# Two-layer hybrid transformer on one core: where modulation is made, and how the last feed-forward chunk fetches and stores its residual

## The chip, the core and the metric

The kernel runs on one NeuronCore of one Trainium2 chip. The metric is the device time of one execution in microseconds (us); the kernel before has a median of 1690.97 us over three runs (1690.32 to 1692.22).

## The reference

Two consecutive layers act on 512 latent tokens and 256 context tokens of width 1024. Every layer does, for both streams,

```python
h = rms_norm(x) * (1 + scale1) + shift1
x = x + gate1 * (attention(h) @ w_out)
h = rms_norm(x) * (1 + scale2) + shift2
x = x + gate2 * (silu(h @ w_gate) * (h @ w_up)) @ w_down
...
out = rms_norm(x_latent) * final_norm
```

The six vectors shift, scale and gate of each layer (called components 0 to 5: shift1, scale1, gate1, shift2, scale2, gate2) are products of a conditioning vector, passed through SiLU, with a 1024 x 6144 matrix. The latent tokens use the vector c (v = 0 in the kernel), the context tokens c_ctx (v = 1). Layer 0 has multi-head latent attention and 2-D neighbourhood attention side by side; layer 1 has sliding-window attention. Only the latent tokens leave layer 1, so in layer 1 the context tokens give keys and values and no more.

## The kernel before

**Layout.** Activations lie transposed: feature on the partitions, token on the free axis. The residual is eight tiles (m = 0 to 7) of 128 features by 768 tokens, of which `LATS` is the first 512 columns and `CTXS` the last 256. The matmuls reach fp32 accuracy by splitting each operand into a rounded part and a remainder: `load_w` (L300) loads weights into a "wr" buffer by SP's queue, ScalarE casts them to "wh" (L305), VectorE or, where the planner's table says so, GpSimd subtracts to get "wl" (L306), and `mm3` (L309) does three matmuls for each pair of tiles (L315 to L317). There are three buffers each of wr, wh and wl, 24 of "b" (768 columns wide), eight of "p", and four each of "ph" and "pl".

**Order.** A scheduler that simulates a time line orders the instructions of each engine; each engine then executes its own list in order. Where no engine is given, `dma` issues on SP's queue, and SP waits in order for whatever a transfer needs, with all later transfers behind it. L133 is the line of that helper, so all such issues have it.

**Modulation.** `mod_tile` (L204) makes one of the eight 128-feature parts of a component. In its late form it loads a 512 KB tile into the only buffer "rope0" and takes one pass of VectorE for each conditioning vector (L214, a multiply with a running sum, and a short read of the sum). `mods_pe` (L178) makes a whole component with TensorE: for each of four steps eight matmuls of 128x256 with a 32-column stationary operand (L190), a copy by ScalarE (L192), two matmuls that pick the two vectors (L194) and two small additions on VectorE (L198). Its weights come in 256 KB loads. `PE_MODS` lists the components that take this way. All other parts are in one queue: of layer 0 the components 2, 4, 3 and 5, then of layer 1 the components 1, 0 and 2, 4, 3, 5. `bg(n)` (L289) makes the next n units of that queue where the program has it; `mod(...)` (L294) makes units until the wanted one is there. `BG` says how many units are made after each tile: `BG[1]` in layer 0's feed-forward (3 for the first four pairs, then 2), `BG[2]` in layer 0's output projection (1 for each latent tile), `BG[3]` in the last feed-forward projections. `DBG` is the pace of such units during layer 0's projections.

**Norm and output projection.** `output` (L1079) loops over two token ranges (latents, then context) and over the eight tiles: load weights, multiply, add to the residual (`add_residual`, L1058), square on ScalarE (L347) and add the squares on VectorE or GpSimd (L350). `rstd` (L353) then sums over the partitions with TensorE (L360), takes the root (L361) and reciprocal (L362), spreads it over a diagonal (L363), broadcasts it with TensorE (L368) and copies it (L369); after that each tile is scaled and shifted (L382 on VectorE, L383 on ScalarE, L384 on VectorE) for the projections that follow. While the second range runs, the first range's norm is taken in steps.

**Layer 0's feed-forward.** `ffn0` (L1255) goes in chunks over pairs j of the hidden dimension. `first_pair` (L1239) does j = 0 in plain form; from j = 1 `Pair` (L1183) uses a scheme with fewer products, with sums of weights made on VectorE (L1199 to L1207, casts L1179, remainders L1180, products and corrections L1217 to L1236). `head`, `body` and `tail` of successive pairs overlap. After each chunk the down projection adds into the residual, which between chunks lies in DRAM as `home[m]`: fetched whole (384 KB), added to, and stored whole.

**The last chunk** calls `output` and writes eight new "b" tiles: since `dst` is given, the latent columns are re-ordered while they are added, by eight small instructions per tile (L1071); the context columns take one (L1066). The old residual is fetched by `fetched` (L1074) at each use: for each tile the latent columns first (256 KB), later the context columns (128 KB), into a "p" buffer. After `ffn0`, the latent columns of each new tile are stored to DRAM (`parked`, L1324 to L1329, 256 KB each); they are read back (L1400 to L1404) for layer 1's output projection. Layer 1's K and V projections come right behind the last chunk (again L315 to L317), and the scheduler interleaves them with it. Since the fetches, the stores and the weights all go by SP's queue, their order there is the scheduler's.

Of the kernel before, what the change touches and what calls it, by code (L numbers as in the profile page):

```python
# [16 lines left out]
KT = D // P  # L17
NL = 512
NX = 256
NT = NL + NX  # L20
# [9 lines left out]
LATS = slice(0, NL)  # L30
CTXS = slice(NL, NT)
HT = NT // 2
TOK1, TOK2 = slice(0, HT), slice(HT, NT)
# [13 lines left out]
QF = 0  # L47
LQ, EACH = 50, 0
NR = "nb"
PE_MODS = ((0, 1), (0, 4))  # L50
SCALES = (2, 0, 1, 0, 1, 0, 0, 0)
KEEP = 1
OUTQ = 1
E0, E1, EF = 1, 1, 1
ORDER = ("2", "n3", "m", "")
AFTER = "012k5678"
DBG = 0.35
KC = (0, 1, 0)
C1 = 0
VP = 0  # L60
# [7 lines left out]
LOWER = 150  # L68
LOE = {(0, 2, 0): None, (0, 2, 1): None, (0, 5, 0): None, (0, 5, 1): 1, (1, 2, 0): None, (1, 2, 1): None, (1, 5, 0): None, (1, 5, 1): None}
PATTERN = ("fbsfbsfbbsfs",) * 3  # L70
BG = ((0, 0, 0, 0, 0), (3, 2), (1, 0), (0, 0))
FIRST = 2000
STEPS = ((2, 3, 4, 4), 5, 3)
HALVES = (slice(0, 256), slice(256, 512))
# [25 lines left out]
def hybrid_kernel(ctx: ExitStack, tc, I, out):  # L100
# [17 lines left out]
    def B(dt=F32, tag="b"):  # L118
        return T(tag, [P, NT], dt)
# [12 lines left out]
    def dma(o, i):  # L132
        return nc.sync.dma_start(f(o), f(i))  # L133

    V, S, G, PE = nc.vector, nc.scalar, nc.gpsimd, nc.tensor
# [153 lines left out]
    def bg(n=1):  # L289

        for _ in range(n):
            next(mods, None)
# [758 lines left out]
    H = []  # L1051
    for k in range(KT):
        t = B()
# [17 lines left out]
            V.scalar_tensor_tensor(d[:, n], o[:, b].rearrange("p (r c) -> p r c", r=8), g,  # L1071
                                   base[:, b].rearrange("p (r c) -> p r c", r=8), op0=ALU.mult, op1=ALU.add)

    def fetched(m, c):  # L1074
        t = B(tag="p")
        dma(t[:, c], home[m][:, c])
        return t

    def output(src, mov, l, comp, streams, norm, units, dst=None, keep=False, base=None):  # L1079

        rest, kept = iter(()), []
        for i, (c, v) in enumerate(streams):
            for m in range(KT):
                w = kept[m] if keep and i else load_w(src(m), len(mov), P, LOE[l, comp, i], "b" if keep else None)
                if keep and i == 0:
                    kept.append(w)
                o = banks([c], PG)
                mm3(o, w, mov)
                add_residual(m, o[0][0], l, comp, v, c, dst and dst[m], base and base(m, c))
                if c is TOK1:  # L1090
                    dma(home[m], H[m])
                norm.add(m, c)
                next(rest, None)
                bg(units[i])
            for _ in rest:
                pass
            rest = norm.rest(norm.acc, c, v)
        for _ in rest:
            pass

    STREAMS0 = ((LATS, 0), (CTXS, 1))
# [63 lines left out]
    norm, ops, sums = combined(H, 0, 3)  # L1165
# [12 lines left out]
    def parts(t, h, lo):  # L1178
        S.copy(h, t)  # L1179
        V.tensor_tensor(lo, t, f(h), op=ALU.subtract)  # L1180
        return h, lo
# [57 lines left out]
    def first_pair(tag):  # L1239

        dst, s = [B(F32R, tag) for _ in range(2)], B(tag="p")
        ws = [load_w(I["w_gu"][0, 0, i], KT, P) for i in range(2)]
        for c, a in ((TOK2, ("12", "22")), (TOK1, ("11", "21"))):
            for i, (h, lo) in enumerate(ws):
                o = PG()[:, :HT]
                for n, k in enumerate((0, 4, 1, 5, 2, 6, 3, 7)):
                    three(o, (h[:, k], lo[:, k]), ops[a[k // 4]][k % 4], n == 0, n == 7)
                if i == 0:
                    S.activation(s[:, c], o, AF.Silu)
                else:  # L1250
                    V.tensor_tensor(s[:, c], s[:, c], o, op=ALU.mult)
                    parts(s[:, c], *(x[:, c] for x in dst))
        return dst

    def ffn0(new, norm):  # L1255
        tags = ("st", "st", "b", "b")
        for ci, (k0, kc) in enumerate(CHUNKS0):
            hs, last = [], None
            for j in range(k0, k0 + kc):
                if j == 0:  # L1260
                    hs.append(first_pair(tags[0]))
                    for _ in sums():
                        pass
                else:
                    p = Pair(j, tags[j - k0])
                    p.head()
                    if last:
                        last.tail()
                    p.body()
                    hs.append(p.dst)  # L1270
                    last = p
                bg(BG[1][j >= 4])
            last.tail()
            src = lambda m: I["w_dn"][0, m, :, k0 * P : (k0 + kc) * P]
            if ci < len(CHUNKS0) - 1:
                for m in range(KT):
                    t = fetched(m, slice(0, NT))
                    o = banks((LATS, CTXS), PG)
                    mm3(o, load_w(src(m), kc, P), hs)
                    for i, (x, c) in enumerate(o):  # L1280
                        add_residual(m, x, 0, 5, i, c, None, t)
                    dma(home[m], t)
            else:
                new.extend(B() for _ in range(KT))
                output(src, hs, 0, 5, STREAMS0, norm, BG[3], new, False, fetched)

    def ffn(l, a, streams, new, norm):
        wide = [c for c, _ in streams] if l == 0 else [LATS]
# [30 lines left out]
    new = []  # L1319
    norm, A = modulated(new, 1, 0, G if E0 else None)  # L1320
    ffn0(new, norm)
    H = new


    parked = []
    for k in range(KT):
        t = dr.tile([P, NL], F32, name=f"parked{k}")
        dma(t, H[k][:, LATS])
        parked.append(t)  # L1329
    rope1 = T("rope0", [P, 2, NL])  # L1330
    dma(rope1, I["rope1"])
# [68 lines left out]
    H = []  # L1400
    for k in range(KT):
        t = B()
# [3 lines left out]
    norm, a = modulated(H, 1, 3, G if E1 else None)  # L1406
# [113 lines left out]
```

## Time and profile before

| what | value |
|---|---|
| median of the runs | 1690.97 us |
| profiled execution | 1692.46 us |
| its span in the profile | 1690.7 us |
| mean granted TensorE clock | 0.969 |

The profile has one execution on one core. PE is TensorE's matmuls, PEld its weight loads, DVE is VectorE, ACT ScalarE, POOL GpSimd, SP the engine that issues most transfers; PEq, SPq and the like are what an engine's sequencer does. A line of a time line has the start in us, the duration in us, the engine, the line of the kernel, the operation, output and inputs with the names of their buffers, the shape, the number of instructions taken together (x), and in brackets how long the engine stood idle before it and who ended that. A line of waits gives the waiting engine and line, the releaser, the sum in us, the number of waits and the longest. PEclk is the clock that was granted to TensorE, 1.00 being full speed.

### The profile page before, as it was taken

Reading aid. Unit: us, or ns where it says so; the run is one execution under the profiler, and the core shown is the slowest. Engines: PE = TensorE matmul, PEld = TensorE weight load, DVE = VectorE, ACT = ScalarE, POOL = GpSimd, SP = SyncE. Lnnn points to the kernel's source line nnn. Section 1 sums busy time; section 2 is a strip of 40 time slices with the busy share of each in tenths; the row PEclk is TensorE's granted clock in tenths of the full one; section 3 lists DMA queues with packets and bytes.
Section 4 is the critical chain, followed back from the end, with each engine's and each line's share of the span. In section 5 each row is a group of like instructions: output and inputs, shape, how many; then the busy total and the mean of one; then the engine's idle time right before and its main releaser. Section 6 shows DMA issues by size and latency. Waiting matters only on the chain. (4 is left out here: it accounts for less than half of the span.)

```text
span 1690.7 us, 24474 instructions
## 1 busy us (share of the span) xinstructions
PE 1565.4 (93%) x9110; PEld 1351.1 (80%) x9110; DVE 1116.0 (66%) x2241; ACT 751.2 (44%) x1466; POOL 257.7 (15%) x192
## 2 busy tenths in 40 slices
PE   4899989999887899999999994799999999999997
PEld 3587767777787789999999994587879888888887
DVE  5994878576889778675858673658887533343435
ACT  5453576675354324242424332447865422222223
POOL 1552722320000000000000003275003000000002
PEclk8899999999998999999999997799999999999999
DMA  9444232004641374646464634332005223232322
GB/s 326 159 152 157 77 109 71 22 6 150 203 171 56 124 280 161 214 142 224 150 215 144 246 122 143 101 100 88 2 2 172 90 83 117 83 104 82 110 70 90
DMA packets 82896, 216.36 MB, mean 128 GB/s; under 512 B 10069, under 2 KB 17753, under 8 KB 82777
## 3 DMA queue, kind: packets, MB, share of 16 engines
q1 hardware_dynamic: 81624, 213.75, 38.4%
q8 instruction: 71, 1.16, 0.3%
q10 hardware_dynamic: 1152, 1.05, 0.2%
q14 instruction: 49, 0.39, 0.1%
HBM read 188.55 MB, written 23.07 MB: 125 GB/s over the span
## 5 line engine op out<-in xcount | busy, mean ns | idle before, releaser
L305 ACT CAST wh<-wr 128x1024 fp32r<-128x1024 f32 (+4 forms) x183 | 156.8, 865 | 393.8 <-PE pss L316 100.7
L306 DVE TENSOR_TENSOR wl<-wr,wh 128x1024 fp32r<-128x1024 f32 (+4 forms) x172 | 182.2, 1065 | 134.5 <-ACT wh L305 131.7
L350 POOL TENSOR_TENSOR p<-p,p 128x256 f32<-128x256 f32 (+1 forms) x42 | 44.9, 1068 | 1131.0 <-DVE wl L306 649.8
L316 PE MATMUL psd<-b,wh 128*128 128x512 f32 (+3 forms) x388 | 139.4, 360 | 3.3 <-DVE b L1180 2.0
L315 PE MATMUL psd<-b,wh 128*128 128x512 f32 (+3 forms) x356 | 131.1, 369 | 7.7 <-DVE b L1066 5.3
L316 PE MATMUL pss<-b,wh 128*128 128x512 f32 (+3 forms) x394 | 136.0, 346 | 1.8 <-DVE b L384 1.8
L317 PE MATMUL psd<-b,wl 128*128 128x512 f32 (+3 forms) x356 | 129.0, 362 | 0.0
L518 ACT ACTIVATE p<-p,sm 128x512 f32<-128x512 f32 (+3 forms) x144 | 105.1, 730 | 35.6 <-DVE sm L522 33.3
L317 PE MATMUL pss<-b,wl 128*128 128x512 f32 (+3 forms) x338 | 119.8, 355 | 0.0
L315 PE MATMUL pss<-b,wh 128*128 128x512 f32 (+3 forms) x338 | 119.6, 357 | 0.0
L214 DVE CUSTOM_DVE_ANT_0 p<-rope,cond 128x1024 bf16<-128x1024 f32 x80 | 96.0, 1221 | 27.6 <-DMA rope<-in_mod_w_dram 27.3
L316 PE MATMUL pst<-b,wh 128*128 128x512 f32 (+2 forms) x274 | 94.5, 345 | 0.2 <-DVE b L1180 0.2
L316 PEld LDWEIGHTS psd<-b,wh 128*128 128x128 f32 (+1 forms) x388 | 73.1, 189 | 15.3 <-DVE b L384 3.3
L315 PE MATMUL pst<-b,wh 128*128 128x512 f32 (+2 forms) x234 | 84.1, 360 | 0.7 <-ACT b L1179 0.7
L317 PE MATMUL pst<-b,wl 128*128 128x512 f32 (+2 forms) x234 | 83.4, 357 | 1.1 <-DVE wl L306 1.1
L315 PEld LDWEIGHTS psd<-b,wh 128*128 128x128 f32 (+1 forms) x356 | 67.2, 189 | 20.7 <-ACT b L383 8.2
L316 PEld LDWEIGHTS pss<-b,wh 128*128 128x128 f32 (+1 forms) x394 | 74.3, 189 | 11.1 <-DVE b L384 2.0
L512 PE MATMUL pso<-ph,b 128*64 128x256 f32 (+1 forms) x384 | 77.9, 361 | 3.5 <-DVE ph L450 3.5
L512 PE MATMUL pso<-pl,b 128*64 128x256 f32 (+1 forms) x384 | 77.3, 360 | 0.2 <-DVE pl L450 0.2
L315 PE MATMUL pst<-st,wh 128*128 128x256 f32 (+2 forms) x161 | 55.2, 343 | 22.4 <-DVE b L1071 21.9
L315 PE MATMUL pss<-st,wh 128*128 128x512 f32 (+2 forms) x217 | 74.3, 342 | 1.4 <-ACT st L339 1.4
L317 PEld LDWEIGHTS psd<-b,wl 128*128 128x128 f32 (+1 forms) x356 | 67.3, 189 | 9.6
(462 smaller groups left out, 4561.8 us busy)
## 6 DMA issues: line engine op xcount, KB each, us to landing
wr<-in_w_gu_dram SPq DMA_DIRECT2D x88, 512.0 KB, 3.5
rope<-in_mod_w_dram SPq DMA_DIRECT2D x56, 512.0 KB, 3.3
wr<-in_w_out_dram SPq DMA_DIRECT2D x32, 512.0 KB, 3.5
p<-home SPq DMA_DIRECT2D x40, 384.0 KB, 5.7
home<-p SPq DMA_DIRECT2D x40, 384.0 KB, 4.2
wr<-in_w_in_dram SPq DMA_DIRECT2D x21, 512.0 KB, 3.4
wr<-in_w_dn_dram SPq DMA_DIRECT2D x32, 256.0 KB, 3.6
ph<-in_mod_w_dram SPq DMA_DIRECT2D x24, 256.0 KB, 3.3
```

The lines of the kernel that those rows point to most:

```text
L214: V.tensor_tensor_reduce(out=T("p", [P, D], mybir.dt.bfloat16), in0=w, in1=cond[:, v, :], op0=ALU.mult, op1=ALU.add, scale=1.0, scalar=0.0 ...
L305: S.copy(h, r)
L306: (G if eng else V).tensor_tensor(lo, r, f(h), op=ALU.subtract)
L315: PE.matmul(o, wh[:, k], mh[:, c], start=first and k == 0, stop=False)
L316: PE.matmul(o, wh[:, k], ml[:, c], start=False, stop=False)
L317: PE.matmul(o, wl[:, k], mh[:, c], start=False, stop=last and k == n - 1)
L350: (eng or V).tensor_tensor(acc[:, :n], acc[:, :n], t[:, :n], op=ALU.add)
L512: ins = PE.matmul(o[64 * i : 64 * i + 64, c], v(kt), t, start=n == 0, stop=n == len(moving[i]) - 1)
L518: S.activation(p[:, c], p[:, c], AF.Exp, bias=nm, scale=-1.0, accum_out=dn)
```

## The change

Five edits:

1. The gate of layer 0's feed-forward, component (0, 5), joins `PE_MODS`. Its steps are made by two `bg(2)`: in `first_pair` after the first half of the tokens (`TOK2`), and after the head of pair 1.
2. `DBG` goes from 0.35 to 0.38.
3. `BG[2]` goes from (1, 0) to (0, 0): no units in layer 0's output projection. `BG[1]` becomes 2 units for each pair with j > 2, and none before apart from the two `bg(2)`.
4. In the last chunk each residual tile is fetched once and whole, into a "b" buffer, ahead of `output`.
5. The parked stores are issued by ScalarE.

In the order of the instructions that comes of it, the L214 go from 80 to 64, none stands in layer 0's output projection, and the first in the feed-forward comes behind the third pair. Layer 1 is left with ten tiles of modulation, where it had one or two: two of component (1, 3), which its output projection's norm needs, and the eight of (1, 5) in its feed-forward. The eight whole fetches follow each other on SP's queue behind the weight load for m = 5 of the last chunk. On ScalarE's list each parked store stands behind the square (L347) of its tile or of the next one, and between the fourth store and the fifth stand three casts of weights (L305).

```diff
-PE_MODS = ((0, 1), (0, 4))
+PE_MODS = ((0, 1), (0, 4), (0, 5))
...
-DBG = 0.35
+DBG = 0.38
...
-BG = ((0, 0, 0, 0, 0), (3, 2), (1, 0), (0, 0))
+BG = ((0, 0, 0, 0, 0), 2, (0, 0), (0, 0))
...
-    def fetched(m, c):
-        t = B(tag="p")
+    def fetched(m, c, tag="p"):
+        t = B(tag=tag)
         dma(t[:, c], home[m][:, c])
         return t
...
     def first_pair(tag):
...
+            if c is TOK2:
+                bg(2)
         return dst
...
     def ffn0(new, norm):
...
                     p.head()
+                    if j == 1:
+                        bg(2)
                     if last:
                         last.tail()
...
-                bg(BG[1][j >= 4])
+                if j > 2:
+                    bg(BG[1])
...
                 new.extend(B() for _ in range(KT))
-                output(src, hs, 0, 5, STREAMS0, norm, BG[3], new, False, fetched)
+                old = [fetched(m, slice(0, NT), "b") for m in range(KT)]
+                output(src, hs, 0, 5, STREAMS0, norm, BG[3], new, False, lambda m, c: old[m])
...
-        dma(t, H[k][:, LATS])
+        S.dma_start(t, H[k][:, LATS])
```

## Prediction

> **What bounds the kernel now.** I began with the page's first parts, then a table of stretches, then the waits of TensorE, and last the time lines of the stretches where TensorE stands still. A row of stretches gives PE, PEld, DVE, ACT and POOL busy time, PEclk, the DMA share and GB/s.
>
> ```profile
> span 1690.7 us, 24474 instructions
> ```
> ```profile
> 460.00:480.00 20.00, 16.04 (x78) 15.78 (x79) 13.89 (x28) 8.58 (x18) 0.00 (x0) 0.83 0.56 198
> 500.00:550.00 50.00, 36.10 (x171) 32.50 (x169) 44.79 (x76) 24.70 (x41) 0.00 (x0) 0.90 0.18 63
> 550.00:600.00 50.00, 42.91 (x227) 37.58 (x228) 38.67 (x71) 14.59 (x29) 0.00 (x0) 1.00 0.47 163
> 1000.00:1050.00 50.00, 29.64 (x143) 25.40 (x142) 20.47 (x74) 12.86 (x25) 12.45 (x11) 0.83 0.45 139
> 1050.00:1104.00 54.00, 42.65 (x188) 34.11 (x189) 35.63 (x59) 23.74 (x42) 15.41 (x14) 0.72 0.28 88
> 1350.00:1650.00 300.00, 300.00 (x1313) 245.86 (x1312) 108.29 (x124) 78.64 (x101) 0.00 (x0) 1.00 0.30 92
> ```
>
> TensorE bounds it: from 1350 to 1650 it never stops, and nothing on another engine can matter there. A gain has to come from its holes. Three lie where the change reaches: 4.0 us in 460 to 480 (the end of layer 0's output projection), 13.9 + 7.1 = 21.0 us in 500 to 600 (the entry of layer 0's feed-forward), 20.4 + 11.4 = 31.7 us in 1000 to 1104 (its last output projection and layer 1's K and V). Their clocks are 0.83 and 0.72 in the last, so work there is stretched as well. Who ends those holes, in the list of TensorE's waits (us in total, times, longest):
>
> ```profile
> PE pst L315 <- DVE b L1071: 21.9, 2, 12.5
> PE pss L360 <- DVE p L350: 6.2, 1, 6.2
> PE psd L315 <- DVE b L1066: 5.3, 1, 5.3
> PE psd L728 <- ACT b L339: 4.6, 1, 4.6
> ```
>
> The profiled execution took 1692.46 us, 1.5 above the median of 1690.97; I sum against 1692.46 and take 1.5 off.
>
> **Part 1, the last output projection (fetch whole, stores on ScalarE).** First the chain as it runs now: VectorE's residual additions L1071, SP's issues and waits, and what a fetch costs.
>
> ```profile
> 1015.58 1.63 DVE L1071 SCALAR_TENSOR_TENSOR b<-pst,mod,p 128x64 f32<-128x64 f32 x8 [0.93 <-PE pst L317]
> ...
> 1050.55 1.62 DVE L1071 SCALAR_TENSOR_TENSOR b<-pst,mod,p 128x64 f32<-128x64 f32 x8 [3.38 <-DMA p<-home]
> ...
> 1061.37 0.85 DVE L382 SCALAR_TENSOR_TENSOR p<-b,mod,nb 128x512 f32<-128x512 f32 x1 [1.02 <-ACT nb L369]
> ...
> 1084.31 0.42 DVE L363 TENSOR_TENSOR p<-ident_r,sm 128x256 f32<-128x256 f32 x1
> 1091.47 3.26 DVE L382 SCALAR_TENSOR_TENSOR p<-b,mod,nb 128x256 f32<-128x256 f32 x8 [6.74 <-ACT nb L369]
> ```
> ```profile
> SPq L133 <- DVE wl L306: 83.8, 15, 26.2
> SPq L133 <- DVE b L1071: 22.9, 7, 6.0
> ```
> ```profile
> 1003.98 7.29 SPq L133 DMA_DIRECT2D wr<-in_w_dn_dram  x2
> 1017.23 0.33 SPq L133 DMA_DIRECT2D parked<-b  x1
> 1017.61 0.42 SPq L133 DMA_DIRECT2D p<-home  x1
> ```
> ```profile
> p<-home SPq DMA_DIRECT2D x8, 256.0 KB, 2.9
> ```
> ```profile
> p<-home SPq DMA_DIRECT2D x40, 384.0 KB, 5.7
> ```
>
> L1071 starts at 1015.58 and, seven tiles later, at 1050.55: (1050.55 - 1015.58)/7 = 5.0 us per tile. It is a ring: L1071 takes 1.63; SP holds the parked store until L1071 is done (1015.58 + 1.63 = 1017.21; the store goes at 1017.23), and only then issues the next fetch (1017.61), which takes 2.9 to land. 1.63 + 0.4 + 2.9 = 4.9. TensorE's part of a tile is far less:
>
> ```profile
> 1014.68 0.40 PE L315 MATMUL psd<-b,wh 128*128 128x512 f32 x1
> 1014.91 0.40 PE L316 MATMUL pst<-b,wh 128*128 128x512 f32 x1
> ...
> 1037.92 0.41 PE L316 MATMUL pst<-st,wh 128*128 128x256 f32 x1
> ...
> 1060.50 0.28 PE L317 MATMUL pss<-st,wl 128*128 128x256 f32 x1
> ...
> 1070.91 0.63 PE L317 MATMUL psd<-b,wl 128*128 128x512 f32 x1
> 1071.34 0.63 PE L315 MATMUL psd<-b,wh 128*128 128x512 f32 x1
> ...
> 1090.36 0.59 PE L368 MATMUL pss<-p,ones 128*128 128x256 f32 x2
> ```
>
> Nine matmuls 0.23 apart (1014.68, 1014.91) are 2.1 us, so eight latent tiles need 17 us.
>
> After, no fetch waits for a tile of this stage: the eight stand on SP behind the weight load of m = 5, which leaves now at 1003.98 + 7.29 = 1011.3 (it waits for L306 to free its buffer). From there eight issues of 0.43 are 3.4 us. They move 3.1 MB; at the 198 GB/s of 460 to 480 the last is there at 1011.3 + 15.9 = 1027, earlier than TensorE asks for tile 7 (1014.7 + 7 x 2.1 = 1029). The cover is thin at the first: if it needs 5.7, it lands at 1017, 1.5 later than L1071 starts now. SP also holds the loads of m = 6 and 7 behind the fetches, and the stores of tiles 3 and 4 on ScalarE wait for fetches 6 and 7 to land, with three casts (m = 6, m = 7, first context tile) queued behind the first of them; those are wanted near 1027, when the fetches land. The parked tiles are read back only for layer 1's output projection. The fetched tiles hold eight more of the 24 "b" buffers, each until its context columns are added, and the norm's results take theirs as those come free: at 5.0 us per tile this costs nothing, at the new pace perhaps 1 to 2 us, which is in the 5 below. I allow TensorE 2 us of stall for all this: last L1071 done at 1014.7 + 17 + 2 + 1.63 = 1035, where it is 1050.55 + 1.62 = 1052.2 now.
>
> What is late next is GpSimd, which adds the squares (L350) and makes weight remainders (L306):
>
> ```profile
> L350 POOL TENSOR_TENSOR p<-p,p 128x512 f32<-128x512 f32 x7 | 8.9, 1270 | 664.4 <-DVE wl L306 649.8 <-ACT p L347 14.6
> L306 POOL TENSOR_TENSOR wl<-wr,wh 128x384 fp32r<-128x384 f32 x8 | 8.1, 1015 | 6.2 <-ACT wh L305 6.2
> ```
>
> In the new order four L306 stand ahead of the last L350: seven L350 and four L306 are 13 us from the second tile's square (its L1071 ends at 1015.58 + 2 x 1.63 = 1019), so 1032 at the least, and the last square is not there before 1035; with casts queued behind stores I take 1038.6. Now, from the end of the last L1071 to the first L382, 1061.4 - 1052.2 = 9.2 us pass, half of it matmuls at low clock; after the last L350 I take 5 of them: first L382 at 1043.5, 18 us earlier. The stretch from there to the context's L363 (1084.31 - 1061.37 = 22.9) loses small waits for fetches: 2 us. Then L382 waits 6.74, for L368 stands in TensorE's order behind K and V matmuls 0.43 apart (1070.91, 1071.34) in place of 0.23: 3 us. **Sum -23.** Bounds: -3, if the ring only changes its links (eight store issues of 0.33 off SP), and -37, if the 31.7 us of holes all go and K and V run at full clock (some 25 matmuls by 0.2 = 5).
>
> A rule speaks against the store's new queue: the Trainium skill, DMA: Bandwidth & Descriptors, section Issuing engines are not separate DMA queues, says that a second issuing engine saves only the sequencer's time to issue, as all run on the same 16 DMA engines. By it the stores' move gives those 8 x 0.33 = 2.6 us. The trace differs in what was held: SP's 22.9 us are not issue time but an in-order wait in which the next fetch stood.
>
> The clock: TensorE's matmuls took 0.41 against 0.28 after the hole of 9.4 (21.9 - 12.5), and 0.63 against 0.40 after that of 5.3. The Trainium skill, TensorE: Matmul & The Clock Gate, section HAM oscillation — how this bites in real kernels, names idle gaps over about 3.4 us as the cause; by it all of this stretch goes to full clock only if no such gap stays, and the trace agrees with both gaps. One may stay, between the context's matmuls (half as wide, some 8.5 us from 1034, so done near 1042) and the first of K and V (first L382 and two more products after 1043.5, so near 1046); I count only part.
>
> **Part 2, no modulation in layer 0's output projection.** L214, which makes a tile of modulation in two passes, as a group in 425 to 475 (first row) and in 500 to 600 (second), and where TensorE waits:
>
> ```profile
> 463.96 1.44 PE L360 MATMUL pss<-ones,p 128*128 128x1 f32 x6 [6.15 <-DVE p L350]
> ```
> ```profile
> L214 DVE CUSTOM_DVE_ANT_0 p<-rope,cond 128x1024 bf16<-128x1024 f32 x14 | 16.6, 1221 | 3.4 <-DMA rope<-in_mod_w_dram 3.4
> ...
> L214 DVE CUSTOM_DVE_ANT_0 p<-rope,cond 128x1024 bf16<-128x1024 f32 x24 | 28.5, 1222 | 12.6 <-DMA rope<-in_mod_w_dram 12.6
> ```
>
> Fourteen L214, 1.22 each, stand on VectorE in 425 to 475, in the way of the L350 that L360 waits 6.15 for. Without them VectorE has 17 us less to do, and L360's wait goes but for one to two us; the clock of 0.83 there recovers part of 3 us more. The norm's next steps are then VectorE's L363 and ScalarE's copy, which were not late. **-5**; bounds 0 (the entry's norm chain ends no earlier) and -9 (6.15 and 3).
>
> **Part 3, the feed-forward's entry.** In 500 to 550 VectorE is busy for 44.79 of 50 us, and 24 L214 take 28.5 us of 500 to 600. TensorE's holes there were 21.0: 4.6 for the norm (L339), the rest mostly VectorE's products. With no L214 before the third pair, of the 16 us of holes behind the first one I let 10 go, and 1 of the norm's. Added to TensorE are four steps of the gate:
>
> ```profile
> 140.68 0.41 PE L190 MATMUL pss<-ph,cond_col 128*32 128x256 f32 x2
> ...
> 141.68 0.50 PE L315 MATMUL psd<-b,wh 128*128 128x512 f32 x1
> ...
> 151.01 0.61 PE L194 MATMUL psd<-pick,p 128*128 128x2 f32 x4
> 151.54 0.41 PE L190 MATMUL pss<-ph,cond_col 128*32 128x256 f32 x2
> ```
>
> L190 of one step: 141.68 - 140.68 = 1.0; L194: 151.54 - 151.01 = 0.5. Four steps are 6.1 us, of which two can lie in the norm's hole. The last two steps' weights go to buffers (ph, pl) that earlier L190 must free, and the pairs share them: up to one load behind each, 3.3 by the 512 KB rows below, and I take 2. So -11 + 4 + 2 = **-5**; bounds -14 (holes gone, steps hidden) and +4 (no hole closes, steps half hidden). Casts, copies (L192) and the gate's small additions (L198) ride on engines that TensorE no longer waits for; the 8 L214 tiles fewer by the gate are off VectorE for good. DBG moves one background step into the projections: nothing.
>
> **Part 4, modulation left for layer 1.** Skipping leaves ten tiles for layer 1 instead of one or two: two are forced by the norm of its output projection, eight go in its feed-forward, where TensorE is at 100% and VectorE at 108 of 300 us: nothing. The loads:
>
> ```profile
> rope<-in_mod_w_dram SPq DMA_DIRECT2D x2, 512.0 KB, 3.3
> ```
>
> The first tile is there long before. The second has the same buffer: it is loaded after the first L214, so VectorE may stand 3.3 + 1.22 with its L306 and L382 behind it. The bounds are 0 and 2 x 1.22 + 3.3 = 5.8, a little more with a slow clock behind it; I take **+3**.
>
> **Sum:** -23 - 5 - 5 + 3 = -30: 1692.5 - 30 = 1662.5, against the median **1661**.
>
> **The rivals.**
> - *The clock recovers and all holes close.* Part 1 at -35 and part 3 at -9: 1691 - 35 - 5 - 9 + 3 = 1645 to 1650. For it: 0.72 in 1050 to 1104. Against it: GpSimd's 13 us chain and the gap before K and V.
> - *Fetches stay slow, a ring of another kind.* Casts behind stores, loads behind fetches: a tile at 3.5 us rather than 5.0 or 2.1. Part 1 at -10: 1674. For it: 5.7 us of the whole fetches, 15 waits of SP for L306. Against: the fetches wait for nothing of this stage.
> - *The stores do no more than save issue time* (part 1 at -3, the change not doing what it says): 1691 - 3 - 5 - 5 + 3 = 1681. Against: SP's 22.9. The rule of the Trainium skill's DMA: Bandwidth & Descriptors, cited in part 1, would expect this one.
> - *Slower: the gate's steps stop TensorE.* Each step stands in TensorE's order; its loads stand in SP's, which waited 83.8/15 = 5.6 us on average for L306. If every step has that and 3.3 of landing, four cost 36 in place of my 6: 1661 + 36 = 1697. It decides from 30/4 = 7.5 us per step more than counted. Against: the first two steps' loads wait for nothing.
>
> **How the numbers follow.** Forecast 1653 to 1669: 0.47. Full recovery: 0.17. Slow fetches 1670 to 1680: 0.20. Issue time only: 0.06. Slower: 0.06; no change, by gains and stops that cancel: 0.04. Range 1645 to 1683: it leaves out the last two and the low edge of the second. A measurement tells about 0.2% (3.4 us) from no change: faster 0.90, same 0.04, slower 0.06.
>
> **What would show it.** L1071 about 2.1 us apart and its waits for home gone; no SP wait for L1071; first L382 near 1043 less the 10 gained before; L360 of layer 0's output waiting under 2 us; L190 in 500 to 530 with waits under 3 us each; one wait of VectorE for rope in layer 1's output projection. The forecast is wrong if TensorE still waits for L1071 for over 5 us, or if L190 waits for loads add up to over 10.

## The result and the profile after

The changed kernel takes 1643.45 us (median of four runs, 1641.44 to 1650.22); in the same session the kernel before took 1691.6. The ratio is 0.9721, with a 95% interval of 0.9692 to 0.9751; a second session of five runs gave 0.9712 (0.9698 to 0.9725). So it is 48 us faster, where 30 were predicted: the direction was right, and the time lies 1.6 us under the range.

The first profiled execution of the changed kernel (1650.22 us) met a stretch of lower TensorE clock in the last chunk, so I read the second one, of span 1641.3. Its table of stretches, with the columns of the one before; what began at 474 us now begins some 12 us earlier, and the last chunk some 25:

```profile
460.00:480.00 20.00, 20.00 (x116) 19.73 (x115) 19.53 (x39) 17.13 (x37) 0.00 (x0) 1.00 0.60 206
500.00:550.00 50.00, 48.77 (x275) 44.34 (x276) 42.06 (x77) 29.34 (x52) 0.00 (x0) 0.94 0.22 69
550.00:600.00 50.00, 50.00 (x289) 45.83 (x288) 32.97 (x57) 13.48 (x24) 0.00 (x0) 1.00 0.67 226
...
1000.00:1050.00 50.00, 42.03 (x197) 34.03 (x196) 37.41 (x84) 25.81 (x49) 24.83 (x22) 0.88 0.40 130
1050.00:1100.00 50.00, 48.54 (x249) 41.27 (x248) 32.64 (x60) 27.74 (x44) 38.15 (x26) 1.00 0.29 95
```
```profile
450.00:475.00 25.00, 25.00 (x146) 24.73 (x146) 18.81 (x36) 16.06 (x32) 0.00 (x0) 1.00 0.53 184
475.00:500.00 25.00, 21.18 (x144) 19.06 (x142) 17.88 (x34) 12.37 (x24) 0.00 (x0) 0.99 0.46 153
```

The reader should see that the hole at the end of layer 0's output projection is gone (none from 450 to 475), and that the last chunk still has holes, and a clock of 0.88. Of the 21.0 us of holes in 500 to 600, 1.2 are left in the same window; but the first hole, the norm's, has moved ahead of 500, so 3.8 + 1.2 = 5.0 is the figure to compare. To size each part I cut the span at three instructions: the first scaling of the feed-forward's norm (L1118), the first latent addition of the last chunk (L1071), and the scaling of layer 1's context tiles (L382 of 256 columns, eight together). The cuts of the changed kernel (of the cuts before, the prediction shows two, and L1118 at 474.18 stands under part 2 below):

```profile
462.27 1.40 DVE L1118 SCALAR_TENSOR_TENSOR b<-b,mod,nb 128x128 f32<-128x128 f32 x4
```
```profile
991.08 1.63 DVE L1071 SCALAR_TENSOR_TENSOR b<-pss,mod,b 128x64 f32<-128x64 f32 x8 [0.93 <-PE pss L317]
...
1008.84 1.62 DVE L1071 SCALAR_TENSOR_TENSOR b<-pss,mod,b 128x64 f32<-128x64 f32 x8 [0.24 <-PE pss L317]
...
1020.09 1.90 DVE L382 SCALAR_TENSOR_TENSOR p<-b,mod,nb 128x512 f32<-128x512 f32 x2 [1.17 <-ACT nb L369]
...
1042.67 3.26 DVE L382 SCALAR_TENSOR_TENSOR p<-b,mod,nb 128x256 f32<-128x256 f32 x8 [3.98 <-ACT nb L369]
```

| us | to L1118 | feed-forward (to L1071) | last chunk (to the context's L382) | rest | span |
|---|---|---|---|---|---|
| before | 474.2 | 541.4 | 75.9 | 599.2 | 1690.7 |
| changed | 462.3 | 528.8 | 51.6 | 598.6 | 1641.3 |
| difference | -11.9 | -12.6 | -24.3 | -0.6 | -49.4 |
| predicted | -5 | -5 | -23 | +3 | -30 |

In the feed-forward's column TensorE's idle time is the length less its busy time (before, then changed): 541.40 - 518.55 = 22.9 us, and 528.81 - 522.52 = 6.3.

```profile
474.18:1015.58 541.40, 518.55 (x2914) 489.79 (x2913) 404.94 (x702) 206.95 (x377) 0.00 (x0) 0.99 0.51 173
```
```profile
462.27:991.08 528.81, 522.52 (x3005) 494.03 (x3004) 393.25 (x687) 209.38 (x383) 0.00 (x0) 0.99 0.52 174
```

### The profile page after: what moved, and what is told of

It is laid out like the page before. It is cut to its first block, busy times and chain, and to the rows that moved or that the text cites. A ratio compares the mean times of both kernels' runs of the same rounds, so it can differ in the third digit from the quotient of the medians.

```text
span 1648.4 us, 24602 instructions
## 1 busy us (share of the span) xinstructions
PE 1566.2 (95%) x9190; PEld 1354.7 (82%) x9190; DVE 1097.4 (67%) x2215; ACT 749.9 (45%) x1470; POOL 257.8 (16%) x192
## 4 chain that ended last, share of the span: by engine, by line
PE 78%; DVE 8%; issue 4%; POOL 2%; DMA 2%; ACT 2%; POOLq 0%; DVEq 0%; ACTq 0%
PE pss L315 6%; PE pss L316 6%; PE pss L317 6%; PE psd L315 5%; PE pso L512 4%; PE psd L316 4%; PE psd L317 4%; PE pst L317 4%; PE pst L315 4%; PE pst L316 4%; PE pss L1174 3%; PE pss L1176 3%; PE pss L1175 3%; PE pst L459 2%; PE psd L459 2%
## 5 line engine op out<-in xcount | busy, mean ns | idle before, releaser
L305 ACT CAST wh<-wr 128x1024 fp32r<-128x1024 f32 (+4 forms) x183 | 157.0, 865 | 386.5 <-PE pst L316 91.7
L306 DVE TENSOR_TENSOR wl<-wr,wh 128x1024 fp32r<-128x1024 f32 (+4 forms) x172 | 184.8, 1078 | 120.1 <-ACT wh L305 115.9
L350 POOL TENSOR_TENSOR p<-p,p 128x256 f32<-128x256 f32 (+1 forms) x42 | 45.1, 1073 | 1090.2 <-DMA b<-home 624.5
L316 PE MATMUL pss<-b,wh 128*128 128x256 f32 (+3 forms) x402 | 138.3, 346 | 0.0
L316 PE MATMUL psd<-b,wh 128*128 128x512 f32 (+3 forms) x373 | 131.5, 353 | 0.0
L315 PE MATMUL psd<-b,wh 128*128 128x512 f32 (+3 forms) x341 | 123.9, 363 | 1.0 <-ACT b L451 1.0
L315 PE MATMUL pss<-b,wh 128*128 128x512 f32 (+3 forms) x346 | 122.9, 359 | 0.8 <-ACT b L1179 0.7
L317 PE MATMUL psd<-b,wl 128*128 128x512 f32 (+3 forms) x341 | 121.8, 357 | 0.0
L316 PE MATMUL pst<-b,wh 128*128 128x512 f32 (+2 forms) x281 | 99.0, 352 | 1.0 <-DVE b L384 1.0
L315 PE MATMUL pst<-b,wh 128*128 128x512 f32 (+2 forms) x241 | 87.7, 365 | 0.0
L214 DVE CUSTOM_DVE_ANT_0 p<-rope,cond 128x1024 bf16<-128x1024 f32 x64 | 76.9, 1219 | 16.1 <-DMA rope<-in_mod_w_dram 15.4
L316 PEld LDWEIGHTS pss<-b,wh 128*128 128x128 f32 (+1 forms) x402 | 77.3, 193 | 9.1 <-DVE b L340 0.2
L315 PE MATMUL pss<-st,wh 128*128 128x256 f32 (+2 forms) x230 | 78.8, 342 | 1.9 <-ACT st L339 1.4
L317 PE MATMUL pss<-st,wl 128*128 128x256 f32 (+2 forms) x230 | 78.6, 342 | 0.0
L316 PEld LDWEIGHTS psd<-b,wh 128*128 128x128 f32 (+1 forms) x373 | 69.8, 187 | 9.1 <-issue 0.2
L315 PEld LDWEIGHTS pss<-b,wh 128*128 128x128 f32 (+1 forms) x346 | 66.5, 193 | 10.9 <-ACT b L1179 1.2
L315 PEld LDWEIGHTS psd<-b,wh 128*128 128x128 f32 (+1 forms) x341 | 63.7, 187 | 12.8 <-issue 2.2
```

What stands on the lines that cost most here:

```text
L214: V.tensor_tensor_reduce(out=T("p", [P, D], mybir.dt.bfloat16), in0=w, in1=cond[:, v, :], op0=ALU.mult, op1=ALU.add, scale=1.0, scalar=0.0 ...
L305: S.copy(h, r)
L306: (G if eng else V).tensor_tensor(lo, r, f(h), op=ALU.subtract)
L315: PE.matmul(o, wh[:, k], mh[:, c], start=first and k == 0, stop=False)
L316: PE.matmul(o, wh[:, k], ml[:, c], start=False, stop=False)
L317: PE.matmul(o, wl[:, k], mh[:, c], start=False, stop=last and k == n - 1)
```

## Experiments

The same three cuts serve for all kernels; "stage" below is the feed-forward's column. Ratios are to the kernel before, with 95% intervals; 0.001 is 1.7 us.

**The changed kernel again.**

> The changed kernel once more. Theory (the last projection's ring broken and VectorE's queue cleared at two places): 1643 us in the timed runs, ratio 0.972. The first profiled execution took 1650.2, about 7 above the other runs of the same kernel. If that was one stretch of low TensorE clock in that execution, this profile lies near 1643 and shows the stretch at full clock; if it is something that the profile does to this kernel, it is near 1650 again.

0.9712 (0.9698 to 0.9725). The stretch 1000 to 1050 of its first profile, to be held against the row with 0.88 above:

```profile
1000.00:1050.00 50.00, 41.90 (x173) 33.37 (x172) 32.64 (x77) 21.56 (x40) 22.70 (x21) 0.74 0.45 146
```

The first profile's last chunk took 56.5 us (992.95 to 1049.46) and this one 51.6: 5 of the 7 us that they differ by.

**The two halves of the change, and one quarter.** The first has only the edits to the last chunk, the second only the others, the third only `BG[2]`.

```diff
tail_only: +old = [fetched(m, slice(0, NT), "b") ...]   +S.dma_start(t, H[k][:, LATS])
mod_only:  +(0, 5) in PE_MODS, DBG 0.38, BG (.., 2, (0, 0), ..), the two bg(2), "if j > 2"
out_only:  -BG = (.., (3, 2), (1, 0), (0, 0))   +BG = (.., (3, 2), (0, 0), (0, 0))
```

> The kernel before with the whole fetches and ScalarE's stores alone. Theory that the parts add: the first profile puts 42.0 us at the context's scaling (L382), of which 22.6 were there when the last output projection began, so this part alone gives 19 us, 1672. Rival that the stage's gain needs the lighter VectorE ahead of it (weights and casts early enough): under 12 us, 1679 or more. Rival that the prediction's 23 was right and the modulation gives the rest: 1668.

> The kernel before with the gate on TensorE, the new units and DBG, without the change at the last output projection. Theory that the parts add: 22.6 us by the first profile, 1669, with layer 1's ten late tiles costing under 1. Prediction's sizes: -5 - 5 + 3, so 1684. Rival that the ring of fetches at the end takes a part of it back (no queue was ahead): 1675.

> The kernel before with only BG[2] set to zero: no modulation in layer 0's output projection, while the gate is still made by VectorE and the feed-forward keeps its three and two units. Theory of a local hole: L360's wait of 6.15 goes and the clock behind it stays full, 8 to 9 us gained, 1682. Rival that VectorE's work is only moved (fourteen L214, 17 us, meet the entry later, where VectorE is at 44.8 of 50 us): no gain or a few us lost, 1690 to 1694.

tail_only 0.9864 (0.9851 to 0.9876), 23 us; mod_only 0.9851 (0.9839 to 0.9864), 25 us; their sum, 48, is what both give together. For tail_only that is the last rival's size, the prediction's 23, and not the 19 of the theory; mod_only gave somewhat more than its theory. tail_only's last chunk took 51.6 us, as in the changed kernel: that part needs nothing of the other. In mod_only the ring is untouched, and TensorE stands in the last chunk as before, its second long wait now ahead of the norm's sum, which stands behind the last addition:

```profile
PE psd L315 <- DVE b L1071: 14.7, 1, 14.7
PE pss L360 <- POOL p L350: 9.6, 1, 9.6
PE pst L315 <- DVE b L1066: 6.5, 1, 6.5
```

out_only 0.9937 (0.9925 to 0.9948), 10.7 us: the fourteen L214 that left the output projection did not come back as a price elsewhere (stage 543.1 against 541.4). DBG was not run alone; out_only, which has the old value, reaches L1118 at 462.31, the changed kernel at 462.27, so no effect of it is seen there. That leaves 25.2 - 10.7 = 14.5 for the feed-forward's entry and layer 1, where the prediction had 2.

**The last chunk's two edits apart.**

> The kernel before with ScalarE's stores alone; the fetches stay in two parts and one by one in the order of the additions. Both tail edits together gave 0.9864, 23 us. Theory that the ring is SP's wait for L1071 in front of the next fetch: without the stores on SP the fetches run ahead through the p buffers, 15 to 23 us gained, 0.987 to 0.991. The rule that a second issuing queue only saves issue time would give 2.6 us: 0.998.

> The kernel before with the whole fetches alone; the stores stay on SP, behind the fetches, with the weight loads of m = 6, 7 and of the context tiles between them. Theory that taking the fetches ahead breaks the ring by itself, while SP still holds weight loads until L1071 of earlier tiles: 12 to 20 us gained, 0.988 to 0.993. If both edits are needed, under 8 us: over 0.995.

stores_only 0.9951 (0.9939 to 0.9964), 8 us; fetch_only 0.9868 (0.9853 to 0.9883), 22 us, which is all that both have together. In stores_only VectorE's additions still wait for fetches, since the fetches stand on SP among the weight loads, each of which waits for L306 of an earlier tile (VectorE's time line, then SP's):

```profile
1027.58 1.62 DVE L1071 SCALAR_TENSOR_TENSOR b<-pss,mod,p 128x64 f32<-128x64 f32 x8 [3.28 <-DMA p<-home]
...
1041.37 1.62 DVE L1071 SCALAR_TENSOR_TENSOR b<-pst,mod,p 128x64 f32<-128x64 f32 x8 [3.84 <-DMA p<-home]
```
```profile
1037.33 0.33 SPq L133 DMA_DIRECT2D wr<-in_w_dn_dram  x1
1037.70 0.94 SPq L133 DMA_DIRECT2D p<-home  x2
```

The fetch of tile 7 leaves at about 1038, behind a weight load, and its L1071 follows at 1041.37. In fetch_only SP still waits for L1071, but only its stores and later weights stand behind that wait:

```profile
SPq L133 <- DVE b L1071: 9.2, 7, 2.6
```

So the whole fetch breaks the ring; the other queue for the stores breaks one of its links (8 us, against 2.6 by issue time alone) and adds nothing measurable once the fetches run ahead. My expectation for stores_only (15 to 23) missed: I had taken the store for the only thing ahead of the next fetch.

**L214 back at the entry, and the gate back on VectorE.** Both start from the changed kernel.

```diff
entry_on: -BG[1] = 2, "if j > 2"    +BG[1] = (3, 2), bg(BG[1][j >= 4]) from pair 0
nogate:   -(0, 5) in PE_MODS, the two bg(2)
```

> The changed kernel, but with units made at the feed-forward's entry as before: (3, 2) from pair 0 on, so that the gate's four steps still go to TensorE and layer 1's parts are made by VectorE from the first pairs. mod_only minus out_only is 14.6 us, where the prediction had 2 for it. Theory that L214 between the first pairs opened nearly all holes there: TensorE waits again for L1180 and the like, 8 to 13 us come back, 1651 to 1656. Rival that the gate's move to TensorE alone did it (sixteen L214 fewer at all): 1643 to 1646.

> The changed kernel without the gate on TensorE (PE_MODS as before, no bg(2) in the first pairs): its eight tiles, two L214 each, now fall between the third pair and the first down projection, which needs them. Theory that a burst through the single 512 KB buffer stops TensorE: eight times a load of 3.3 and two L214 of 1.3 are 47 us, of which two pairs' time covers a part: 10 to 35 us slower than the changed kernel, 1653 to 1678. Rival that VectorE has the room there (slices of 65% busy): within 3 us of 1643.

entry_on 0.9838 (0.9823 to 0.9853), 21 us over the changed kernel: more than the theory said, and not the rival. TensorE's time line, 525 to 565, where the changed kernel has no wait at all:

```profile
526.77 0.69 PE L1176 MATMUL pss<-b,wl 128*128 128x384 f32 x1 [3.31 <-DVE wl L1180]
548.09 0.44 PE L1174 MATMUL psd<-st,wh 128*128 128x384 f32 x1 [1.11 <-ACT wh L1179]
...
559.98 0.69 PE L1174 MATMUL pss<-st,wh 128*128 128x384 f32 x1 [6.95 <-ACT p L1224]
```

nogate 0.9829 (0.9812 to 0.9846), 20 us over it. The burst stops TensorE once, at the first down projection:

```profile
592.99 0.58 PE L315 MATMUL psd<-st,wh 128*128 128x256 f32 x1 [13.30 <-DVE p L1066]
```

Its stage took 541.9, 13 over the changed kernel; another 5 were there at L1118 already (467.3), and the profiled execution (1669.56, where the median is 1664.03) lost 8 more behind the stage, neither of which I followed. TensorE's idle time in the stage is 22.9 us in entry_on and 22.6 in nogate, as in the kernel before (22.9), and 6.3 with both edits. So it takes both: the gate must be off VectorE, and what is left must come later. In nogate the idle time lies elsewhere, 13.3 of it at the first down projection.

**A third unit per pair.** `BG[1]` = 3 instead of 2, so that nothing is left for layer 1.

> The changed kernel with three units for each pair from the third on instead of two: all of layer 1's modulation is then made in layer 0's feed-forward, none late. The prediction's +3 for the two forced tiles in layer 1's output projection says 1640. The profile of the changed kernel (42.0 us ahead at the context's L382 and 42.2 at the end) says 0 to 1: 1642 to 1644, if the third unit hides in the feed-forward. Rival that the third unit opens holes there: 1646 or more.

0.9759 (0.9738 to 0.978), 8 us over the changed kernel; the rival was right. The rest behind the last chunk took 596.1 us, 2.5 less than in the changed kernel, but the stage 539.6, 10.8 more, and the last chunk 54.0, 2.4 more. In it VectorE's L214, first in the changed kernel from 620 on, then in this one:

```profile
L214 DVE CUSTOM_DVE_ANT_0 p<-rope,cond 128x1024 bf16<-128x1024 f32 x43 | 51.7, 1220 | 14.2 <-DMA rope<-in_mod_w_dram 14.1
```
```profile
L214 DVE CUSTOM_DVE_ANT_0 p<-rope,cond 128x1024 bf16<-128x1024 f32 x50 | 60.5, 1225 | 40.4 <-DMA rope<-in_mod_w_dram 40.2
```

Busy time rose by 8.8 us, the idle time ahead of L214, waiting for its load, by 26. That made a theory: L214 costs not only its 1.22 us but its wait, in order, for a tile that can be loaded into the only buffer after the L214 before has read it.

**Without that wait.** First by letting L214 read resident data in entry_on and after_bg3:

```diff
-tensor_tensor_reduce(.., in0=w, in1=cond[:, v, :], ..)
+tensor_tensor_reduce(.., in0=cond[:, 1 - v, :], in1=cond[:, v, :], ..)
```

> entry_on (0.9838 of the kernel before, about 20 us over the changed kernel) with L214 reading the resident conditioning vectors instead of the tile that it has loaded; every load and every L214 is still there, but none waits for a load. It leaves out the modulation matrix of the parts that VectorE makes, so its output is not the reference's. In entry_on's 420 to 640, L214 is busy for 38 us and waits 15.9 for its loads. Theory that the wait in order behind the only buffer is a large part of the price: half or more of the 20 us goes, ratio 0.972 to 0.978. Rival that the busy time alone does it: 0.981 to 0.984.

> after_bg3 (0.9759, some 8 us over the changed kernel) with the same edit: L214 reads what is resident, every load is still issued; the output is not the reference's. In after_bg3, L214 waits 39.2 us for its loads in 640 to 1000, against 14.1 in the changed kernel, at the same busy time per unit. Theory that a third unit costs by its wait for the single buffer: 0.969 to 0.972, all of the 8 us gone. Rival that VectorE is simply full: 0.975.

0.9982 (0.9973 to 0.9991) and 0.9898 (0.9881 to 0.9915): both slower than the kernels they came from, and of no use as totals. With no reader to wait for, SP issued the tile loads early, and a weight load of layer 0's output projection stood behind twelve of them; TensorE stood for it (entry_on_nowait, SP and TensorE):

```profile
381.98 38.81 SPq L133 DMA_DIRECT2D rope<-in_mod_w_dram  x12
420.90 0.37 SPq L133 DMA_DIRECT2D wr<-in_w_out_dram  x1
```
```profile
426.41 0.69 PE L315 MATMUL pss<-b,wh 128*128 128x384 f32 x1 [28.61 <-ACT wh L305]
```

The stages behind it can be compared: 543.4 against 550.5 of entry_on, 530.3 against 539.6 of after_bg3. So I made a second buffer instead; the room comes from one "p" buffer, so the changed kernel with the same edit is the control.

```diff
-late.append(lambda: T("rope0", [P, D]))
+late.append(late_tile)
-p=8
+p=7
```

> after_bg3 (three units per pair; 0.9759, first additions of the last chunk 539.6 us behind the first scaling of the feed-forward's norm, against 528.8 in the changed kernel) with two buffers in turn for the modulation tiles, and seven p buffers in place of eight to make room. Theory that a third unit costs by L214's wait in order for the one buffer (39.2 us in 640 to 1000): the stage goes back to 529 to 532 and the ratio to 0.970 to 0.973. Rival that VectorE's busy time is the price: stage 538 or more, ratio 0.975.

> entry_on (0.9838; the stage 550.5 us) with two buffers in turn and seven p buffers. Without the wait (entry_on_nowait) the stage took 543.4, a third of the 21.7 us less, though its time as a whole was spoilt by loads that ran ahead of the weights in the projection before. Theory that two thirds of the price at the entry are busy time in the place where VectorE is full, and one third the wait: stage 542 to 546, ratio 0.978 to 0.981. Rival that it is all wait: stage under 534, ratio under 0.975.

> The changed kernel with two buffers in turn and seven p buffers: the control for the other two. If seven p buffers cost nothing and the 14.1 us of waiting for loads in 640 to 1000 lie beside other work (TensorE is at 100% there): 0.970 to 0.972, the same as the changed kernel. If the p buffers are short: 0.974 or more.

| | ratio | stage, one buffer | stage, two buffers |
|---|---|---|---|
| two units (control after_two) | 0.9749 (0.9736 to 0.9762) | 528.8 | 527.5 |
| third unit (bg3_two) | 0.9745 (0.9731 to 0.9759) | 539.6 | 527.8 |
| L214 at the entry (entry_on_two) | 0.9789 (0.977 to 0.9808) | 550.5 | 536.9 |

The control itself is some 5 to 6 us slower than the changed kernel, all of it outside the stage; it has two edits, the second buffer and the missing "p", and no run has the second alone. Against it a third unit is free, where it cost 10.8 us of stage with one buffer: by the stages that price was the wait alone. The entry's price falls from 21.7 to 9.4 us of stage: 12.3 are the wait, 9.4 stay with no wait for a load:

```profile
L214 DVE CUSTOM_DVE_ANT_0 p<-rope,cond 128x1024 bf16<-128x1024 f32 x24 | 28.5, 1226 | 15.9 <-DMA rope<-in_mod_w_dram 15.9
```
```profile
L214 DVE CUSTOM_DVE_ANT_0 p<-rope,cond 128x1024 bf16<-128x1024 f32 x28 | 33.0, 1212 | 0.0
```

(entry_on up to 620, then entry_on_two.) bg3_two's stage came out as the theory had it, and its ratio did not, because the two edits together are not free, as after_two shows. entry_on_two lies between its theories: somewhat over half of the price is the wait, where a third was expected.

**Three tries for a better version.** after_lat moves the context's L306 of the last chunk to VectorE (`LOE[0, 5, 1]` from 1 to None); after_e0_lo moves the latents' L306 to GpSimd too and the squares' sums (L350) to VectorE (`E0` 0, `LOE[0, 5, 0]` 1); bg3_two_h3 is bg3_two with its room from "ph" and "pl" (three each) and eight "p".

> The changed kernel with the weight remainders (L306) of the last context tiles on VectorE instead of GpSimd. The changed profile has TensorE waiting 7.1 us for GpSimd's L350 in all. Theory that GpSimd's chain ends the norm late: 2 to 4 us faster, 1639 to 1641. Rival that VectorE, with eight more L306 of 0.55 each between its residual additions, is later by as much: 1643 to 1647.

> The changed kernel with GpSimd and VectorE changing places in the last chunk: GpSimd makes all weight remainders (L306), VectorE adds the squares (L350). In the changed kernel's last chunk TensorE waits 6.0 us for VectorE's L306, which stand behind three residual additions, and 2.8 for GpSimd's L350. Theory that the wait for L306 was the cost of the order on VectorE: 3 to 6 us faster, 0.968 to 0.969. Rival that GpSimd's L306 of 1.0 us each, eight more of them, set a pace of their own: 0.972 or more.

> Two buffers for the modulation tiles and three units per pair as in bg3_two, but the room comes from ph and pl (three each in place of four), with the eight p buffers kept. bg3_two lost about 4 us ahead of layer 0's output projection, which its seven p buffers would explain, and its feed-forward stage (527.8) was as short as that of the control. Theory: nothing is lost ahead of it, no late tile is left for layer 1 (2.6 us by the profiles of after_bg3 and entry_on against the changed kernel), so 1639 to 1641, 0.968 to 0.970. Rival that ph and pl, which carry the gate's weights and the pairs' sums, now make TensorE wait at the entry: 0.973 or more.

after_lat 0.9708 (0.9691 to 0.9724) and after_e0_lo 0.9712 (0.9698 to 0.9726) are the changed kernel within the interval. In the latter TensorE's wait for VectorE's L306 in 975 to 1060 falls from 6.0 to 2.3 us, and others take its place (changed kernel, then after_e0_lo):

```profile
PE pst L317 <- DVE wl L306: 6.0, 2, 3.5
PE pss L360 <- POOL p L350: 2.8, 2, 2.3
```
```profile
PE pst L316 <- DVE b L384: 3.2, 3, 2.2
PE pss L360 <- DVE p L350: 3.0, 1, 3.0
PE pst L315 <- ACT wh L305: 2.7, 1, 2.7
PE pst L317 <- DVE wl L306: 2.3, 1, 2.3
```

bg3_two_h3 is slower, 0.9813 (0.9797 to 0.9829), with a stage of 541.8: the rival's side, though I did not trace it to a single wait; L214's waits for loads are 1.1 us in its stage, so they are not the reason. Its theory that nothing is lost ahead missed too: with eight "p" buffers it reaches L1118 at 467.9, after_two with seven at 468.0, the changed kernel at 462.3. So that the "p" buffer is what the control lost is not shown; tile loads that run ahead of weights are the rival, and three "ph" and "pl" may do it here. No version beat the changed kernel.

## Why the prediction was right in direction and short in size

By the cuts the forecast was 19.4 us short: 1.3 in part 1, 6.9 in part 2, 7.6 in part 3 and 3.6 in part 4. The time fell under the range by the terms of parts 2, 3 and 4.

**Part 1, the last chunk: right.** Forecast -23, measured -24.3 by the cuts and 23 us alone (tail_only). The steps: L1071 2.5 us apart ((1008.84 - 991.08)/7; forecast 2.1, before 5.0), its waits for fetches gone, SP's wait for L1071 gone. From the first L1071 to the first L382 it is 29.0 us in place of 45.8, 16.8 less for a forecast of 18; from there to the context's L382 22.6 in place of 30.1, 7.5 less for 5. Where 2 us of stall were allowed TensorE waits 3.5, for a reason not named: three L306 stand on VectorE behind the additions of the first three tiles. GpSimd's sum ends the norm, as forecast:

```profile
996.83 0.50 PE L317 MATMUL pst<-st,wl 128*128 128x512 f32 x1 [3.49 <-DVE wl L306]
...
1013.69 1.05 PE L360 MATMUL pss<-ones,p 128*128 128x1 f32 x8 [2.31 <-POOL p L350]
```

The casts queued behind ScalarE's stores did little harm: TensorE waits 0.4 us for one in this chunk. The credit was shared wrongly, though: the argument rested as much on the stores' queue as on the fetches, and fetch_only shows that the fetches do it. The rule from the Trainium skill (DMA: Bandwidth & Descriptors, Issuing engines are not separate DMA queues), which spoke against the stores' new queue, came near the truth once the fetches run ahead, where that queue adds nothing measurable; alone it gave 8 us, more than issue time, because SP holds transfers in order.

**Part 2, the output projection: the mechanism right, the size wrong.** Forecast -5, measured -11.9 by the cut and 10.7 us alone (out_only). One step that failed is "The norm's next steps are then VectorE's L363 and ScalarE's copy, which were not late". L363 was. VectorE before, and the changed kernel:

```profile
465.73 0.18 DVE L362 RECIPROCAL sm<-sm 128x3 f32<-128x3 f32 x1 [1.83 <-ACT sm L361]
467.81 1.22 DVE L214 CUSTOM_DVE_ANT_0 p<-rope,cond 128x1024 bf16<-128x1024 f32 x1 [1.91 <-DMA rope<-in_mod_w_dram]
...
470.11 0.55 DVE L363 TENSOR_TENSOR p<-ident_r,sm 128x384 f32<-128x384 f32 x1
...
474.18 1.40 DVE L1118 SCALAR_TENSOR_TENSOR b<-b,mod,nb 128x128 f32<-128x128 f32 x4
```
```profile
454.69 0.72 PE L360 MATMUL pss<-ones,p 128*128 128x1 f32 x6
```
```profile
455.75 0.18 DVE L362 RECIPROCAL sm<-sm 128x3 f32<-128x3 f32 x1 [0.78 <-ACT sm L361]
455.96 0.56 DVE L363 TENSOR_TENSOR p<-ident_r,sm 128x384 f32<-128x384 f32 x1
```

Before, L363 stood behind two L214, of which the first waited 1.91 us for its load, and so 4.4 us behind L362; now it is 0.2. ScalarE's copy L369, behind a cast, gives part of that back: L360 to L1118 took 474.2 - 464.0 = 10.2 us, after it 462.3 - 454.7 = 7.6. L360 itself comes 9.3 us earlier: its wait of 6.15 is zero, where one to two were to stay; 2.8 come from TensorE's order, in which 180 matmuls stand between layer 0's attention and L360, before 195; and 0.3 from earlier stages. With the 2.6 behind L360 that is the 11.9. Neither L363's place nor the shorter way to L360 was in the forecast, nor in its bound of -9 (6.15 of the wait and 3 of the clock).

**Part 3, the entry: the term that was mis-sized most.** Forecast -11 + 4 + 2 = -5, measured -12.6 for the stage. The step that failed is "of the 16 us of holes behind the first one I let 10 go": nearly all went. TensorE's idle time in the stage fell by 16.6 us (22.9 to 6.3). Its busy time rose by 4.0 (518.55 to 522.52), which is what the forecast counted for the gate's four steps, and -16.6 + 4.0 is the -12.6. The +2 for the steps' weights came to 0.75. Of the norm's hole 4.3 us are left in two waits, the first for ScalarE's copy of a gate step:

```profile
497.47 1.05 PE L194 MATMUL pss<-pick,p 128*128 128x2 f32 x8 [2.34 <-ACT p L192]
500.48 0.69 PE L728 MATMUL psd<-b,wh 128*128 128x384 f32 x1 [1.96 <-ACT b L339]
...
520.57 0.41 PE L190 MATMUL pss<-pl,cond_col 128*32 128x256 f32 x2 [0.75 <-DMA pl<-in_mod_wp_dram]
```

For 10 of the 16 the prediction gives no reason, and what it left out stood in a row that it quotes. It took from it the 28.5 us for which L214 is busy; the same row ends with 12.6 us of idle time ahead of it, waiting for its load. On an engine that works in order, that wait holds back everything behind it, as the busy time does. entry_on against entry_on_two shows its share: 12.3 of 21.7 us. No run takes the wait alone out of the kernel before, so that it has the same share there is inferred. The rival in which the gate's steps stop TensorE had no substance: the one wait for their weights is 0.75.

**Part 4, layer 1: +3 forecast, nothing measured.** The rest is 0.6 us shorter than before. The step that failed is "VectorE may stand 3.3 + 1.22 with its L306 and L382 behind it": the second forced tile's L214 comes 5.0 us behind the first, with other work of VectorE between, and neither waits for its load. In all of layer 1 VectorE waits 0.6 us for one, in the feed-forward.

```profile
1239.70 1.22 DVE L214 CUSTOM_DVE_ANT_0 p<-rope,cond 128x1024 bf16<-128x1024 f32 x1
...
1244.67 1.62 DVE L214 CUSTOM_DVE_ANT_0 p<-rope,cond 128x1024 bf16<-128x1024 f32 x1
```

after_bg3 and bg3_two, without late tiles, have a rest 2.5 and 0.5 us shorter than their controls; but after_e0_lo, with all ten, is at 597.0, and tail_only, with the few of the kernel before, at 600.6. So a price of the late tiles is not shown.

The measured total came near the rival of full recovery (1645 to 1650), which had 0.17, but not by its terms: the last chunk kept holes and a low clock (0.88 in 1000 to 1050), and parts 2, 3 and 4 made up for it.

## What to carry to other kernels

An instruction on an engine that works in order costs its own duration and its wait for its own load; both stand in one row of the groups, and a single buffer turns the second into a price for all that is queued behind. It is a price only where that engine holds others up: with two units per pair the second buffer took the 14.2 us of waits in the row above away, and the stage became 1.3 us shorter. When a stall is to go, follow the chain behind it to its next link and look what else of the removed kind stands there. A ring through a queue is broken best where it can start early (here the fetches), and each link should be undone alone before the credit is shared.

## What the hardware showed that was not expected

The same program gave two lengths of the last chunk, 51.6 us with a granted clock of 0.87 in it and 56.5 with 0.76. Over all kernels here with whole fetches it lies between these two, so a few us between two profiles' totals say little, and the stage is the better measure. TensorE waits of up to 3.5 us are left in the chunk, so whether the clock falls may hang on small shifts; what decides it was not tried.

The eight whole fetches came faster than the 198 GB/s that I had taken from 460 to 480. In the DMA view of the changed kernel from 975 to 1060, in 40 slices of 2.1 us, the seventh to the twelfth (988 to 1000) carry them, the first stores and a few weights at 279 to 400 GB/s. The eight were issued from 986.8 to 990.9 and took at most 8.9 us to land, so all were there within 13.0 us, where 15.9 were forecast:

```profile
GB/s 85 229 107 3 0 20 324 279 389 334 400 359 240 52 221 250 227 215 95 96 69 367 153 231 27 231 66 181 245 10 0 0 0 0 0 0 0 93 235 166
```
